# A gated hybrid block on one core: a new written order, a refitted transfer model and 17 convolution taps moved from VectorE to ScalarE and adding transfers

## The chip, the core and the metric

The kernel runs on one core of a Trainium2 chip. The core has a matrix engine (TensorE, PE in the profile, whose weight loads the profile lists apart as PEld), three engines for elementwise work (VectorE = DVE, ScalarE = ACT, GpSimd = POOL) and SyncE (SP), which here only issues transfers. Each engine works through its own queue in order; an instruction that waits for another engine holds up everything behind it in its queue. The metric is the device time of one execution in microseconds (us).

## The reference

One decoder layer for 256 tokens with 16 meta tokens in front (272 rows), width 2048, float32:

```
u = rms_norm(h, g_pre_mix)
z_pool | v_conv | g_conv | gate_a | gate_b = split(u @ w_in)     # 1024 | 1024 | 1024 | 2048 | 2048 columns
y_a = causal_multiscale_pool(z_pool, w_grp, scale) @ w_pool_out
y_b = conformer_conv(v_conv, g_conv, ...) @ w_conv_out           # a = v*sigmoid(g); 31 causal taps per channel; LayerNorm; silu
m = sigmoid(gate_a) * y_a + sigmoid(gate_b) * y_b
h = h + rms_norm(m @ w_o, g_post_mix)
f = square(relu(rms_norm(h, g_pre_mlp) @ w_up)) @ w_down         # 2048 -> 8192 -> 2048
out = (h + rms_norm(f, g_post_mlp))[16:]
```

## The kernel before

**Products.** A weight matrix is read in chunks of 1 MB (128 partitions x 2048 numbers). Precision comes from splitting: ScalarE rounds a chunk to `hi` (L816), VectorE subtracts to get the rest, `lo` (L821), and each product is made of three matmuls: weight hi with activation hi and lo, and weight lo with activation hi. The chunk lands in a raw room by a transfer that SP issues (L795). There are three pairs of `hi` and `lo`, used in turn, so the `hi` of a product can be written only when the product three places earlier has ended on PE.

**Stages.** Zones come first: eight column strips of `w_in` for z (pool), v and g (convolution), two chunks each, in the order g0, v0 and then the table `AFTER_G0` (L34). From v and g of a zone h come two channel tiles of `a = v*sigmoid(g)` (L939), and from them the convolution: tap 0 with the bias by ScalarE (L944), then for each of the other 30 taps a pair of VectorE instructions that add `tap * shifted a` onto `c` (L951). Then `grp`, the small product of the pool branch, whose result ScalarE (L1069) and VectorE (L1072) take out of the banks as `y`. After it come the products that the table `MAIN` (L36) lists, one word each.

**Words.** `p` is the pool projection, `a` gate a, `b` gate b, `c` the conv projection, `o` is `w_o`. `a13` is the normal product of gate a, column block 1, row block 3: two halves of 12 matmuls, one for each 128 tokens. `a0P5` is one of the seven products of a Strassen scheme over the column blocks 0 and 1; it has 12 matmuls, but its weights are often a sum of two blocks. `T01` transposes a finished block; `fu` makes the Strassen sums of the activations u (L1395, L1165ff, L1177, L1179), `k1` frees a room, `lnm` and `lnv` are the LayerNorm's mean and variance, and the other words are side steps of the same kind.

**Sums of weight blocks.** P5, P6, P7 and P4 need the sum of two blocks. The table `SUMMED` (L42) names those for which both blocks are loaded and VectorE adds them (L833); for the others POOL issues a transfer that reads the second block from memory and adds it onto the first in its room (L837, called a bring here).

**Banks.** There are six PSUM banks for products, four named `bank_k` and two `acc_v`. A Strassen product that goes to two places is copied out by ScalarE (L1300), and a next product that adds into the same bank waits for that copy: in the order before, `a13` follows `a0P5` into the same bank.

**Who sets the order.** The order of PE is the written one. For the other engines the class `Plan` simulates the program: it gives each operation a due time, counted back from the PE product that needs it, and lets an engine take the ready operation with the earliest due time. Transfers have a model of their own: issue time, a moving time, and shares of the bandwidth between SP's and POOL's queues:

```
class Plan:      ISSUE = {"SP": (0.4, 1.09), "POOL": (1.28, 2.44)}; LANDS = 1.13; SHARE SP (1.0, 1.0, 1.0), POOL 3.55
class LoadedPlan: ISSUE = {"SP": (0.4, 1.36), "POOL": (1.28, 2.05)}; LANDS = 0.93; SHARE SP (1.0, 2.54, 4.08), POOL 3.66
```

`LoadedPlan` stands in the kernel before, but no plan uses it. A second plan (L1721) does the same for the MLP, where weights are split at L1799 and L1804, summed at L1816 and L1821, and half of a bank of up-products is taken out by ScalarE (L1876) and the other by VectorE (L1883).

**Moved taps.** `convolve` already has a way for taps that VectorE does not do: for the first `MOVED_TAPS[h]` taps of zone h, ScalarE multiplies both channel tiles into one of three buffers w (L957) and POOL issues a transfer of 256 KB inside the core's memory that adds the buffer onto `c` (L967). The buffers lie in the room S1, next to z. In the kernel before the table is empty. The step `fu` writes its sums into the same room, so its first instruction waits for whoever used it.

Of the kernel before, what the change touches and what calls it, by code (L numbers as in the profile page):

```python
# [30 lines left out]

DUMMIES = (11, 2, 1)
SQUARES_FROM = 5
AFTER_G0 = [("z", 0), ("z", 1), ("z", 2), ("z", 3), ("v", 1), ("g", 1), ("v", 2), ("g", 2),  # L34
            ("v", 3), ("g", 3)]
MAIN = (  # L36
# [5 lines left out]
SUMMED = {('gate0', 0): '67', ('gate0', 2): '57', ('gate1', 0): '5', ('co', 2): '46', ('o', 0): '46'}  # L42
MOVED_TAPS = {}


class Plan:
# [163 lines left out]
def hybrid_block(ctx: ExitStack, tc: tile.TileContext, ins: dict, out: bass.AP):  # L210
    nc = tc.nc
# [393 lines left out]
                self.tile = self.make()  # L605
            return self.tile

    plan = Plan()

    def on_vector(n, f, reads, writes, extra=0.0):  # L610
        plan.add("DVE", (n + 151) / 960 - 0.083 + extra, f, reads=reads, writes=writes, late=0.1)
# [170 lines left out]
    def loads():  # L782
        while to_load:
            r = to_load[0]
            ends_ = uses[last_use[r]][0]
            fit = [q for q in free_rooms if index_of.get(q, len(products)) > ends_]
            if not fit:
                return
            to_load.pop(0)
            q = room_at[r] = fit[0]  # L790
            free_rooms.remove(q)
            src, (rows, _) = source(r)

            def f(q=q, src=src, rows=rows):
                nc.sync.dma_start(rooms[q]().rearrange("p (k c) -> p k c", k=rows), src)  # L795
            if early[0]:
                early[0] -= 1
                f()
            else:
                plan.add("SP", 3.06 if r[0] in ZONES else 2.87, f, writes=(f"raw{q}",))  # L800

    slot0 = at["slot"] - 1
    split_at = [dict() for _ in products]
# [21 lines left out]
    def weights(m_):  # L825
        while done_uses[0] < len(uses) and uses[done_uses[0]][0] <= m_:
            n = done_uses[0]
            done_uses[0] += 1
            w, what, raws_, extra = uses[n]
            at_rooms = [room_at[r] for r in raws_]  # L830
            names = [f"raw{q}" for q in at_rooms]
            if what == "sum":
                plan.add("DVE", 2.22, lambda a=at_rooms[0], b=at_rooms[1]: nc.vector.tensor_add(  # L833
                    rooms[a](), rooms[a](), rooms[b]()), reads=names, writes=names[:1], late=0.13)
            elif what == "bring":
                src, (rows, _) = source(extra)
                plan.add("POOL", 4.94, lambda a=at_rooms[0], src=src, rows=rows: nc.gpsimd.dma_start(  # L837
                    rooms[a]().rearrange("p (k c) -> p k c", k=rows), src, accum_op=ALU.add),
                    reads=names, writes=names)
            else:  # L840
                high, low = split_of(w, at_rooms[0], source(raws_[0])[1][0])
                h_, l_ = half_names(w)
                plan.add("ACT", 1.82, high, reads=names, writes=(h_,), late=0.13)
                plan.add("DVE", 2.22, low, reads=names + [h_], writes=(l_,), late=0.13)
            for r in raws_:
                if last_use[r] == n:
                    free_rooms.append(room_at[r])
            loads()
# [869 lines left out]
    banks["b"] = misc_tile("bank_b")  # L1718
    ov = out[0].rearrange("(t p) d -> p t d", p=P)

    plan = Plan()  # L1721
    steps = []
    for i in range(NP):
        text = FIRST_PIECE if i == 0 else PIECE if i < NP - 1 else LAST_PIECE
# [504 lines left out]
```

## Time and profile before

| | |
|---|---|
| median of 3 runs | 1186.25 us (1184.76 to 1186.58) |
| profiled execution | 1186.12 us |
| its span in the profile | 1184.0 us, 15794 instructions |
| granted TensorE clock, mean | 0.996 |
| PE busy | 1168.2 us (99%) |
| DVE / ACT / POOL busy | 1062.6 / 707.1 / 63.6 us |

The profiled execution lies 0.13 us under the median, and 2.12 us of it lie outside the span. A row of a timeline gives the start, the duration, the engine, the line, the operation, what is written from what, how many instructions are grouped, and in brackets the idle time before them with what ended it. The view of waits sums these idle times by the one who waited and the one waited for. In the chain of work each row is followed back to what released it, so its rows add up to the span. `PE acc_v L1251` is the matmul of a main product into an `acc_v` bank.

### The profile page before, as it was taken

Reading aid. Unit: us, or ns where it says so; the run is one execution under the profiler, and the core shown is the slowest. Engines: PE = TensorE matmul, PEld = TensorE weight load, DVE = VectorE, ACT = ScalarE, POOL = GpSimd, SP = SyncE. Lnnn points to the kernel's source line nnn. Section 1 sums busy time; section 2 is a strip of 40 time slices with the busy share of each in tenths; the row PEclk is TensorE's granted clock in tenths of the full one; section 3 lists DMA queues with packets and bytes.
Section 4 is the critical chain, followed back from the end, with each engine's and each line's share of the span. In section 5 each row is a group of like instructions: output and inputs, shape, how many; then the busy total and the mean of one; then the engine's idle time right before and its main releaser. Section 6 shows DMA issues by size and latency. Waiting matters only on the chain.

```text
span 1184.0 us, 15794 instructions
## 1 busy us (share of the span) xinstructions
PE 1168.2 (99%) x6314; PEld 1013.8 (86%) x6314; DVE 1062.6 (90%) x1154; ACT 707.1 (60%) x718; POOL 63.6 (5%) x63
## 2 busy tenths in 40 slices
PE   9999999999999999999999999999999999999996
PEld 9999988788888888898888888888888888888885
DVE  6799999999989999687998998998989989989856
ACT  7634354565479666466776665666656756656632
POOL 1000000000000000000101001000000010010000
PEclk9999999999999999999999999999999999999998
DMA  9855355898868799449999999999998999999931
GB/s 313 262 181 180 107 168 175 232 295 277 238 188 258 235 323 334 129 155 333 254 317 233 250 314 259 252 286 245 302 262 228 342 233 249 311 253 247 323 137 71
DMA packets 185705, 288.62 MB, mean 244 GB/s; under 512 B 4785, under 2 KB 92273, under 8 KB 184720
## 3 DMA queue, kind: packets, MB, share of 16 engines
q1 hardware_dynamic: 160496, 235.88, 58.0%
q0 software_dynamic: 24384, 50.49, 23.7%
q10 hardware_dynamic: 752, 1.25, 0.3%
q8 instruction: 49, 0.80, 0.3%
q14 instruction: 24, 0.20, 0.0%
HBM read 283.41 MB, written 4.19 MB: 243 GB/s over the span
## 4 chain that ended last, share of the span: by engine, by line
PE 89%; DVE 5%; DMA 3%; ACT 1%; issue 1%; DVEq 0%; POOL 0%; POOLq 0%; ACTq 0%; SPq 0%
PE bank_k L1251 18%; PE bank_u L538 16%; PE acc_up L1978 12%; PE acc_v L1251 9%; PE bank_u L544 8%; PE bank_a L1978 7%; PE bank_k L533 6%; PE bank_b L1978 5%; PE acc_v L533 3%; DVE c L951 2%; DVE lo L821 1%; DMA kept<-h 1%; PE acc_v L1511 1%; PE bank_u L1978 1%; DMA raw_h<-in_w_up_dram 1%
## 5 line engine op out<-in xcount | busy, mean ns | idle before, releaser
L538 PE MATMUL bank_u<-m,hi 128*128 128x512 f32 x960 | 329.9, 390 | 0.7 <-DVE F_raw L1883 0.7
L544 PE MATMUL bank_u<-m,lo 128*128 128x256 f32 x960 | 265.4, 276 | 0.0
L538 PEld LDWEIGHTS bank_u<-m,hi 128*128 128x128 f32 x960 | 180.2, 188 | 38.9 <-DVE F_raw L1883 1.0
L816 ACT CAST hi<-raw_p 128x2048 fp32r<-128x2048 f32 x70 | 133.8, 1913 | 116.5 <-PE bank_k L533 23.5
L1804 DVE TENSOR_TENSOR lo<-raw_m,hi 128x2048 fp32r<-128x2048 f32 x75 | 171.6, 2288 | 18.8 <-ACT hi L1799 17.7
L544 PEld LDWEIGHTS bank_u<-m,lo 128*128 128x128 f32 x960 | 180.2, 188 | 1.6
L1799 ACT CAST hi<-raw_m 128x2048 fp32r<-128x2048 f32 x75 | 143.4, 1913 | 60.2 <-PE bank_u L538 38.8
L821 DVE TENSOR_TENSOR lo<-raw_p,hi 128x2048 fp32r<-128x2048 f32 x70 | 159.6, 2287 | 16.3 <-ACT hi L816 16.0
L1978 PE MATMUL acc_up<-hi,forms 128*128 128x512 f32 x440 | 143.9, 390 | 0.2 <-ACT G L2003 0.2
L1804 DVE TENSOR_TENSOR lo<-raw_h,hi 128x2048 fp32r<-128x2048 f32 x43 | 98.4, 2287 | 13.3 <-ACT hi L1799 13.1
L1799 ACT CAST hi<-raw_h 128x2048 fp32r<-128x2048 f32 x43 | 82.1, 1910 | 40.5 <-PE bank_u L538 17.8
L951 DVE SCALAR_TENSOR_TENSOR c<-a,taps,c 128x256 f32<-128x256 f32 x240 | 100.3, 479 | 0.0
L1978 PEld LDWEIGHTS acc_up<-hi,forms 128*128 128x128 f32 x440 | 82.6, 188 | 18.4 <-ACT G L2003 0.6
L533 PE MATMUL bank_k<-u_um,hi 128*128 128x272 f32 x512 | 95.2, 287 | 0.0
L1251 PE MATMUL bank_k<-hi,u_um 128*128 128x512 f32 x280 | 88.8, 389 | 0.0
L1978 PE MATMUL acc_up<-lo,forms 128*128 128x512 f32 x220 | 85.9, 391 | 0.0
L1978 PE MATMUL bank_a<-hi,forms 128*128 128x512 f32 (+1 forms) x256 | 81.9, 383 | 0.0
L533 PEld LDWEIGHTS bank_k<-u_um,hi 128*128 128x128 f32 x512 | 79.7, 188 | 0.0
L533 PE MATMUL bank_k<-u_um,lo 128*128 128x272 f32 x256 | 73.3, 287 | 0.0
L1799 ACT CAST hi<-raw_c 128x2048 fp32r<-128x2048 f32 x23 | 43.9, 1908 | 42.0 <-PE bank_u L538 37.1
L1804 DVE TENSOR_TENSOR lo<-raw_c,hi 128x2048 fp32r<-128x2048 f32 x23 | 52.6, 2286 | 13.2 <-ACT hi L1799 13.2
L1978 PE MATMUL bank_b<-hi,forms 128*128 128x512 f32 (+1 forms) x200 | 63.5, 381 | 0.0
(384 smaller groups left out, 2228.8 us busy)
## 6 DMA issues: line engine op xcount, KB each, us to landing
raw_p<-in_w_in_dram SPq DMA_DIRECT2D x32, 1024.0 KB, 5.3
raw_m<-in_w_down_dram SPq DMA_DIRECT2D x25, 1024.0 KB, 8.7
raw_m<-in_w_down_dram POOLq DMA_DIRECT2D x23, 1024.0 KB, 10.3
raw_h<-in_w_up_dram SPq DMA_DIRECT2D x20, 1024.0 KB, 8.0
raw_m<-in_w_up_dram SPq DMA_DIRECT2D x17, 1024.0 KB, 8.5
raw_h<-in_w_down_dram SPq DMA_DIRECT2D x17, 1024.0 KB, 8.9
raw_c<-in_w_down_dram SPq DMA_DIRECT2D x15, 1024.0 KB, 5.1
raw_a<-in_w_up_dram SPq DMA_DIRECT2D x13, 1024.0 KB, 8.2
```

Of the source, the lines that this page charges most:

```text
L533: nc.tensor.matmul(acc, w[:, k[0], cs], act[:, k[1], a, off:], start=first and n == 0, stop=last and n == 2)
L538: nc.tensor.matmul(acc.rearrange("p (a t) -> p a t", a=2)[:, :, ts], hi[:, k[0], cs], act[:, k[1], :, off + ts.start:off + ts.stop], start ...
L544: nc.tensor.matmul(acc[:, :T], lo[:, k[0], cs], act[:, k[1], 0, off:], start=False, stop=stop, skip_group_check=True)
L816: nc.scalar.copy(box["flat"], rooms[q]())
L821: nc.vector.tensor_sub(lo, rooms[q](), f32(box["flat"]))
L951: nc.vector.scalar_tensor_tensor(C_c()[:, q, :], A_a()[:, q, i:i + T], taps[:, q, i:i + 1], C_c()[:, q, :], op0=ALU.mult, op1=ALU.add)
L1251: nc.tensor.matmul(banks[bank], a_(k, part), box[w_][:, k, :], start=opens and k == 0 and i == 0, stop=ends_ and k == CK - 1 and i == 2, s ...
L1511: nc.tensor.matmul(acc, act(kk)(a_, half(t)), w_[:, k, :], start=kk == 0 and n == 0, stop=kk == nk - 1 and n == 2, skip_group_check=True)
L1799: nc.scalar.copy(box["flat"], raw_in(room))
L1804: nc.vector.tensor_sub(lo, raw_in(room), f32(box["flat"]))
L1978: nc.tensor.matmul(acc, forms[h][:, f, k, a_, :], box[w_][:, k, cs], start=start and k == 0 and n == 0, stop=stop and k == KH - 1 and n == ...
```

## The change

Six tables and costs are changed; no instruction is written in another way.

- Both plans use `LoadedPlan`, with costs of 3.15 and 2.95 in place of 3.06 and 2.87 for SP's loads and 5.38 in place of 4.94 for a bring.
- `AFTER_G0`: the strip z3 moves from before v1 to behind v2.
- `MAIN`: the same 96 words in another order.
- `SUMMED`: P6 of gate a's second pair goes from a bring to a VectorE sum, and in the pairs of `w_conv_out` and `w_o` another two of the four are summed.
- `MOVED_TAPS`: 4 taps of zone 1 and 13 of zone 2 go the way of L957 and L967.

```diff
-AFTER_G0 = [("z", 0), ("z", 1), ("z", 2), ("z", 3), ("v", 1), ("g", 1), ("v", 2), ("g", 2),
+AFTER_G0 = [("z", 0), ("z", 1), ("z", 2), ("v", 1), ("g", 1), ("v", 2), ("z", 3), ("g", 2),
             ("v", 3), ("g", 3)]
 MAIN = (
-    "p00 p01 p30 p31 p21 p20 fu p10 p11 k1 a0P1 a0P2 a2P1 a0P5 a13 a12 a0P6 a0P3 a0P7 a02 a0P4 "
...
+    "p00 p30 p31 fu p11 p20 p10 p01 p21 k1 a0P1 a0P2 a0P5 a2P1 a12 a2P2 a0P6 a0P3 a0P7 a03 a0P4 "
...
-SUMMED = {('gate0', 0): '67', ('gate0', 2): '57', ('gate1', 0): '5', ('co', 2): '46', ('o', 0): '46'}
-MOVED_TAPS = {}
+SUMMED = {('gate0', 0): '67', ('gate0', 2): '567', ('gate1', 0): '5', ('co', 2): '67', ('o', 0): '67'}
+MOVED_TAPS = {1: 4, 2: 13}
...
-    plan = Plan()
+    plan = LoadedPlan()
...
-                plan.add("SP", 3.06 if r[0] in ZONES else 2.87, f, writes=(f"raw{q}",))
+                plan.add("SP", 3.15 if r[0] in ZONES else 2.95, f, writes=(f"raw{q}",))
...
-                plan.add("POOL", 4.94, lambda a=at_rooms[0], src=src, rows=rows: nc.gpsimd.dma_start(
+                plan.add("POOL", 5.38, lambda a=at_rooms[0], src=src, rows=rows: nc.gpsimd.dma_start(
...
-    plan = Plan()
+    plan = LoadedPlan()
     steps = []
```

Counted over the whole program, VectorE has 34 tap instructions fewer (206 for 240) and one weight sum more (10 for 9), ScalarE has 34 multiplications more, and POOL issues 17 adding transfers of 256 KB more and one bring fewer (10 for 11). SP's loads stay 240 and PE's instructions 6309, of the same kinds. In the MLP the orders of PE, SP and POOL stay as they were; only VectorE's and ScalarE's change, by a few places near its start. Lines of the changed kernel are one higher than before from L44 on.

**At grp (VectorE).** Before, from the last taps ahead of grp's results on; `acc_v` and `bank_k` hold those results, and `lo_1875` belongs to the second product after grp:

```order
L951 SCALAR_TENSOR_TENSOR c<-a,taps,c 128x256 x4
L821 TENSOR_TENSOR lo_1875<-raw_p_414,hi_1847 128x2048
L1072 SCALAR_TENSOR_TENSOR y<-acc_v_0_169,vecs,y 128x256
L1072 SCALAR_TENSOR_TENSOR y<-acc_v_1_170,vecs,y 128x256
L1072 SCALAR_TENSOR_TENSOR y<-bank_k_406,vecs,y 128x256
L1072 SCALAR_TENSOR_TENSOR y<-bank_k_407,vecs,y 128x256
```

The changed kernel at the same place, where `lo_1913` is that product's:

```order
L952 SCALAR_TENSOR_TENSOR c<-a,taps,c 128x256 x4
L1073 SCALAR_TENSOR_TENSOR y<-acc_v_0_169,vecs,y 128x256
L1073 SCALAR_TENSOR_TENSOR y<-acc_v_1_170,vecs,y 128x256
L1073 SCALAR_TENSOR_TENSOR y<-bank_k_406,vecs,y 128x256
L1073 SCALAR_TENSOR_TENSOR y<-bank_k_407,vecs,y 128x256
L822 TENSOR_TENSOR lo_1913<-raw_p_414,hi_1859 128x2048
L1073 SCALAR_TENSOR_TENSOR y<-bank_k_408,vecs,y 128x256
```

Four of grp's results now stand ahead of the `lo`, two behind it.

**At the first products of gate a (ScalarE, then POOL).** Before, from the `hi` of a0P1 (`hi_2163`) on; `hi_2201` is a0P2's, `hi_2241` a2P1's, `hi_2263` a0P5's, `hi_2283` a13's and `hi_2299` a12's; the copy of a0P5's bank is the one from `acc_v_1_170`:

```order
L816 CAST hi_2241<-raw_p_414 128x2048
L1219 COPY ya<-bank_k_407 128x512
L816 CAST hi_2263<-raw_p_412 128x2048
L1300 COPY sg_2265<-bank_k_408 128x512
L816 CAST hi_2283<-raw_p_413 128x2048
L816 CAST hi_2299<-raw_k_2239 128x2048
L1300 COPY sg_2265<-acc_v_0_169 128x512
L1300 COPY sg_2265<-acc_v_1_170 128x512
```

The changed kernel; `hi_2272` is a0P5's, `hi_2289` a2P1's, `hi_2293` a12's, `hi_2326` a2P2's, and a0P5's bank is `bank_k_406`:

```order
L817 CAST hi_2272<-raw_p_412 128x2048
L817 CAST hi_2289<-raw_p_414 128x2048
L817 CAST hi_2293<-raw_p_413 128x2048
L1301 COPY sg_2309<-acc_v_0_169 128x512
L1301 COPY sg_2309<-bank_k_406 128x512
L817 CAST hi_2326<-raw_k_2262 128x2048
L1301 COPY sg_2309<-bank_k_407 128x512
```

The copy that the product after a0P5's bank needs now stands ahead of the split of `raw_k`, not behind it, and a2P1 lies between the two on PE.

POOL before, from the clearing of `a` on, and then changed; `raw_p_412` holds a0P1's block, onto which the first bring adds for a0P5:

```order
L892 MEMSET a 128x8x14
L837 DMA raw_p_412<-in_w_in_dram 128x4x512 x2
L837 DMA raw_p_414<-in_w_in_dram 128x4x512 x2
L837 DMA raw_p_413<-in_w_in_dram 128x4x512
L837 DMA raw_p_414<-in_w_in_dram 128x4x512 x2
```

```order
L893 MEMSET a 128x8x14
L968 DMA c<-z 128x512 x17
L838 DMA raw_p_412<-in_w_in_dram 128x4x512 x2
L838 DMA raw_p_414<-in_w_in_dram 128x4x512
L838 DMA raw_p_412<-in_w_in_dram 128x4x512
```

The 17 tap transfers stand ahead of the first bring.

**At the start of the MLP (VectorE).** Before; `bank_u` holds up-products:

```order
L1804 TENSOR_TENSOR lo_4875<-raw_a,hi_4851 128x2048
L1883 TENSOR_TENSOR F_raw<-half_1_4873,bank_u_4483 128x256
L1816 TENSOR_TENSOR raw_m_4481<-raw_m_4481,raw_m_4480 128x2048
L1804 TENSOR_TENSOR lo_4896<-raw_m_4479,hi_4892 128x2048
L1883 TENSOR_TENSOR F_raw<-half_1_4894,bank_u_4484 128x256
L1804 TENSOR_TENSOR lo_4919<-raw_m_4481,hi_4915 128x2048
```

The changed kernel:

```order
L1805 TENSOR_TENSOR lo_4871<-raw_a,hi_4868 128x2048
L1884 TENSOR_TENSOR F_raw<-half_1_4891,bank_u_4500 128x256
L1956 TENSOR_TENSOR forms_4490<-F_raw,forms_4490 128x4x128
L1817 TENSOR_TENSOR raw_m_4498<-raw_m_4498,raw_m_4497 128x2048
L1956 TENSOR_TENSOR forms_4491<-F_raw,forms_4491 128x4x128
L1884 TENSOR_TENSOR F_raw<-half_1_4911,bank_u_4501 128x256
L1805 TENSOR_TENSOR lo_4934<-raw_m_4496,hi_4909 128x2048
L1805 TENSOR_TENSOR lo_4936<-raw_m_4498,hi_4932 128x2048
```

The second L1883 (L1884 now) stands ahead of a `lo` that it stood behind, and two steps of L1955 have come in between.

More of the change, by code (lines that the diff above doesn't have):

```diff
@@ L33 @@
 SQUARES_FROM = 5
-AFTER_G0 = [("z", 0), ("z", 1), ("z", 2), ("z", 3), ("v", 1), ("g", 1), ("v", 2), ("g", 2),
+AFTER_G0 = [("z", 0), ("z", 1), ("z", 2), ("v", 1), ("g", 1), ("v", 2), ("z", 3), ("g", 2),
             ("v", 3), ("g", 3)]
 MAIN = (
[5 rows of a table removed]
-SUMMED = {('gate0', 0): '67', ('gate0', 2): '57', ('gate1', 0): '5', ('co', 2): '46', ('o', 0): '46'}
-MOVED_TAPS = {}
[5 rows of a table added]
+)
+SUMMED = {('gate0', 0): '67', ('gate0', 2): '567', ('gate1', 0): '5', ('co', 2): '67', ('o', 0): '67'}
+MOVED_TAPS = {1: 4, 2: 13}
 class Plan:
```

8 rows, old and new, of the table MAIN are left out of this document.

## The prediction

> **What bounds the kernel.** I read the page's busy times first, then PE's waits, then busy times by stage, and the chain and timelines only at the places where PE waits.
>
> ```profile
> span 1184.0 us, 15794 instructions
> PE 1168.2 (99%) x6314; PEld 1013.8 (86%) x6314; DVE 1062.6 (90%) x1154; ACT 707.1 (60%) x718; POOL 63.6 (5%) x63
> ```
>
> PE is the bound. The change leaves its instructions as they are in number and kind, so it can win only what PE waits, and can lose without such a limit. The waits of PE (who waited, for whom, us in total, times, longest):
>
> ```profile
> PE acc_v L1251 <- ACT sg L1300: 1.9, 1, 1.9
> PE idle L450 <- POOL ident masks.py:199: 1.4, 1, 1.4
> PE bank_u L538 <- DVE F_raw L1883: 0.7, 1, 0.7
> PE acc_v L533 <- DVE y L1072: 0.4, 1, 0.4
> PE acc_up L1978 <- ACT G L2003: 0.2, 1, 0.2
> ```
>
> The second lies in the start-up, which isn't touched. The other four make 1.9 + 0.7 + 0.4 + 0.2 = 3.2 us, and that is the most a new order can take off. Busy time by stretches (start and end, length, each engine's busy time, clock, DMA share, GB/s) shows where they lie:
>
> ```profile
> 24.00:156.80 132.80, 132.80 (x1076) 132.39 (x1077) 125.08 (x202) 60.36 (x62) 0.19 (x1) 1.00 0.58 186
> 156.80:163.30 6.50, 6.10 (x50) 5.90 (x49) 6.50 (x13) 5.48 (x10) 0.00 (x0) 1.00 0.53 179
> 163.30:206.80 43.50, 43.50 (x193) 35.99 (x193) 43.50 (x73) 22.07 (x21) 1.37 (x1) 1.00 0.58 180
> 206.80:219.60 12.80, 10.90 (x50) 8.68 (x48) 11.60 (x15) 9.58 (x8) 0.00 (x0) 1.00 0.91 289
> 219.60:375.90 156.30, 156.30 (x688) 129.09 (x689) 148.31 (x151) 95.82 (x80) 8.93 (x7) 1.00 0.82 239
> ```
>
> The zones (first row), the pool products (third) and the rest of the gates (last) run with PE never waiting; the 0.4 us is at grp (second row), the 1.9 us at the first products of gate a (fourth). VectorE is full in rows two and three, but nothing there waits for it beyond the 0.4.
>
> **The 0.4 us at grp.** VectorE takes grp's results out of the banks behind a split:
>
> ```profile
> 158.85 2.29 DVE L821 TENSOR_TENSOR lo<-raw_p,hi 128x2048 fp32r<-128x2048 f32 x1
> 161.05 0.87 DVE L1072 SCALAR_TENSOR_TENSOR y<-acc_v,vecs,y 128x256 fp32r<-128x256 f32 x2
> ```
>
> In the new order four of these results come first. The split's product is the second after grp, so 2.29 us later is still in time. The term is −0.4, as long as ScalarE, whose half of each result comes first, isn't held up by a tap ahead of it (see the tap chain).
>
> **The 1.9 us at a13.** The chain of work (start, length, what):
>
> ```profile
> 195.94 10.89 PE bank_k L1251 x48
> 206.85 9.43 DMA raw_k<-in_w_in_dram
> 216.67 1.91 ACT hi L816
> 218.58 0.97 ACT sg L1300 x2
> ```
>
> The load of `raw_k` starts when the last pool product ends; ScalarE's split of it waits for the landing, and the copy that frees a0P5's bank waits behind the split. Now the copy stands ahead of that split, a2P1 fills 2.7 us between a0P5 and a12, and `raw_k` is first used one product later, by a2P2. The term is −1.9.
>
> **A new wait at a0P5.** This is the term I am least sure of. a0P5 needs a0P1's block with a second one added by a bring, and the rows of before give its whole path:
>
> ```profile
> 195.98 1.92 ACT L816 CAST hi<-raw_p 128x2048 fp32r<-128x2048 f32 x1 [2.13 <-PE acc_v L1251]
> 198.38 2.29 DVE L821 TENSOR_TENSOR lo<-raw_p,hi 128x2048 fp32r<-128x2048 f32 x1
> 200.97 1.37 POOL L837 DMA_DIRECT2D raw_p<-in_w_in_dram  x1 [164.31 <-DVE lo L821]
> 210.09 1.91 ACT L816 CAST hi<-raw_p 128x2048 fp32r<-128x2048 f32 x1 [0.83 <-DMA raw_p<-in_w_in_dram]
> 212.12 2.29 DVE L821 TENSOR_TENSOR lo<-raw_p,hi 128x2048 fp32r<-128x2048 f32 x1
> 212.10 0.39 PE L1251 MATMUL acc_v<-hi,u_um 128*128 128x512 f32 x1
> 214.82 0.39 PE L1251 MATMUL acc_v<-hi,forms_u 128*128 128x512 f32 x1
> DMA to landing us min/median/max: 8.3/9.0/9.7
> ```
>
> The first split cannot start earlier, because its buffer is free only when the sixth of the eight pool products ends. In before the `lo` was ready at 214.41 and a0P5 began at 214.82, its second matmul, the first to read `lo`, 0.23 us behind it. Now a0P5 stands where a2P1 began, 214.82 − 212.10 = 2.72 us earlier: its second matmul is due at 212.32. The first `lo` need not sit behind eight taps now (six stand ahead of it) and can start at 197.90; then it ends at 200.19, the bring starts at 200.5, lands 9.1 us later as here, and 1.91 + 2.29 us and short gaps follow: 213.85. The wait is 1.5 us. With the fastest landing of the last row, 8.3, it is 0.7; with the slowest, 9.7, and the `lo` no earlier than before, it is 2.7. I take 1.5, since this very transfer took 9.1 in this place, beside the same kind of SP loads. [...]
>
> **The tap chain.** Each of the 13 tap transfers of zone 2 adds onto the same `c`, so each waits for the one before. The room the buffers lie in is taken by `fu`'s sums on VectorE, right behind a0P1's `lo`, at about 200.2. The second half of zone 2's `a` is ready at 137.8, and its products have as many ahead of them as before:
>
> ```profile
> 137.37 0.43 DVE L939 TENSOR_TENSOR a<-v,g 128x272 f32<-128x272 f32 x1
> L944 ACT ACTIVATE c<-a,vecs,taps 128x256 f32<-128x256 f32 x8 | 4.7, 594 | 4.2 <-DVE a L939 4.2
> L951 DVE SCALAR_TENSOR_TENSOR c<-a,taps,c 128x256 f32<-128x256 f32 x240 | 100.3, 479 | 0.0
> q0 software_dynamic: 3696, 7.34, 29.7%
> raw_p<-in_w_in_dram POOLq DMA_DIRECT2D x7, 1024.0 KB, 9.2
> 457.42 0.57 POOL L1444 DMA_DIRECT2D g_mix<-in_g_post_mix_dram  x1 [15.84 <-issue]
> out_dram<-F_raw ACTq DMA_DIRECT2D x1, 256.0 KB, 2.4
> taps_in<-in_w_dw_dram POOLq DMA_DIRECT2D x1, 124.0 KB, 6.6
> ```
>
> Two ScalarE multiplications (nearest row L944, 0.59 us) and an issue put the first at 139.1, so 13 transfers have 200.2 − 139.1 = 61.1 us, or 4.7 each. No row of before shows such a transfer. An estimate: in the 145 us from 195 on, seven brings kept the DMA engines 29.7% busy, 6.15 us each, and took 9.2 to land, so 3.05 us are not moving. A quarter of 6.15 is 1.54; a transfer of whole rows is issued in 0.57 instead of 1.27 us; 0.3 for waking POOL (the bring's issue at 200.97 came so long after its `lo` at 200.67) makes 4.2. The ends are 2.4 (256 KB going out) and 6.6 (124 KB, POOL's queue). At 4.2 the last lands at 193.7, and the chain costs nothing. Beyond 4.7 every 0.1 costs 1.3 us, at 6.6 some 25. Beyond much the same value grp's results are late too, since ScalarE holds the seventh tap of zone 2 ahead of them until the fourth transfer has landed; that isn't added, as what PE loses there moves the chain's deadline along.
>
> Zone 1's four taps end long before zone 2 begins. The 34 multiplications (34 x 0.59, at most 20 us) fall on ScalarE, which is 60% busy. VectorE loses 34 x 0.42 (100.3 / 240), 14 us, and gains one sum of 2.3. That wins nothing by itself: PE doesn't wait for the convolution.
>
> ```profile
> 319.89 0.42 DVE L1082 TENSOR_TENSOR v<-v,c 128x256 f32<-128x256 f32 x1
> 334.18 0.59 PE L1094 MATMUL bank_y<-v,ones 128*128 128x256 f32 x2
> ```
>
> The last sum for the mean is done 14 us before PE uses it. In the new order that use comes some 6.5 us earlier and the work is 12 us less, so the cover stays. The moved z3 lies in the zones, where PE never waits: nothing.
>
> **The other order of products and sums.** Among the gates the loads of blocks for a sum now stand closer to their use: counted by these durations, a0P3 (its `lo` stands on VectorE behind a0P7's sum, which needs a second load) and a03 have 0 to 0.3 us to spare, the rest 2 us and more. I put 0 on it, between 0 and +1.
>
> **The MLP's start.** VectorE's second half-bank:
>
> ```profile
> 571.98 0.41 DVE L1883 TENSOR_TENSOR F_raw<-half,bank_u 128x256 f32<-128x256 f32 x1
> 574.51 2.28 DVE L1804 TENSOR_TENSOR lo<-raw_m,hi 128x2048 fp32r<-128x2048 f32 x1
> 576.71 0.41 DVE L1883 TENSOR_TENSOR F_raw<-half,bank_u 128x256 f32<-128x256 f32 x1
> ```
>
> It now comes ahead of the 2.28 us split, so the 0.7 goes; but that split is then late by 0.6 us for two steps of L1955, of which its product bears most. I take −0.5, between −0.7 and +0.3.
>
> **The sum.** −0.4 − 1.9 + 1.5 + 0 + 0 − 0.5 = −1.3. The profiled execution goes from 1186.12 to 1184.8; it lies 0.13 under the median, so the median goes from 1186.25 to 1184.9, or −0.11%. A difference under 0.2% (2.4 us) can hardly be told from none here, so this counts as the same.
>
> **The rivals.**
> - *The bring is early enough.* If it lands in under 8 us, a0P5 waits 0.4 or less, and with the MLP's 0.7 gone the sum is −0.4 − 1.9 + 0.4 − 0.7 = −2.6: 1183.6, just faster; at most −3.2, 1183.0. For it speaks that the bring can start 0.5 us earlier; against it that none of this line landed under 8.3.
> - *The tap chain is too slow (the slower side).* At 5.1 us a transfer, 13 x 0.4 = +5.2 come on top of −1.3: 1190.2. It decides from 5.0 on, where 13 x 0.3 passes 2.4 + 1.3. For it speaks that the chain is strictly serial and that 6.6 stands in the trace; against it that the 6.6 falls into the start, when all loads begin.
> [...]
> - *Late blocks among the gates.* a0P3, a03 or a32 wait for a load or a sum, +1 to +4: 1186 to 1189.
>
> **How the numbers follow.** The forecast, 1184 to 1187 with small misses, 0.39; the early bring 0.36; the slow tap chain 0.14, the starved one 0.02; late blocks 0.09, half of it within 0.2%. So faster 0.36, same 0.43, slower 0.21. From 1182.8, below which the waits of before leave almost nothing, the range reaches to a tap transfer of 5.1 us, 1190.2, and leaves out the slower chains.
>
> **What would show it.** PE's waits lose the entries on L1300, L1072 and L1883 (one line higher now); a new one on `lo` of about 1.5 us stands near 212. The tap transfers show a median of 4.2 us to landing, the last before 195, and VectorE has no idle time ahead of L1396. A landing above 4.7 with VectorE idle there, or PE waiting for grp's banks at 158 to 163, proves the forecast wrong on the slow side; a0P5 on time, on the fast side.

## The result, and the profile after

The changed kernel takes 1197.34 us (median of 5, 1194.41 to 1204.51) where the kernel before, beside it, takes 1186.08: a ratio of 1.0103, with a 95% interval of 1.0087 to 1.0118. It is 1% slower. The forecast was 1184.9, and the range ended at 1190.2. Timed once more on another occasion the ratio was 1.0058 (1.0036 to 1.0080), from executions between 1188.6 and 1199.4: the changed kernel scatters by some 10 us, where the one before scatters by 2 to 6.

The page of the changed kernel, whose lines are one higher than before:

```profile
span 1197.6 us, 15834 instructions
PE 1174.0 (98%) x6314; PEld 1017.5 (85%) x6314; DVE 1052.3 (88%) x1121; ACT 720.3 (60%) x752; POOL 76.8 (6%) x79
```

The span is 13.6 us longer; this execution, of 1199.38 us, lies 2 us above the median. PE's waits:

```profile
PE bank_k L1252 <- ACT ya L1220: 3.1, 2, 2.2
PE acc_v L1252 <- DVE lo L822: 3.1, 1, 3.1
PE bank_k L1252 <- DVE lo L822: 2.0, 1, 2.0
PE acc_v L534 <- DVE y L1073: 1.4, 1, 1.4
PE idle L451 <- POOL ident masks.py:199: 1.4, 1, 1.4
PE bank_k L1252 <- ACT hi L817: 0.5, 1, 0.5
PE acc_up L1979 <- ACT G L2004: 0.4, 1, 0.4
PE bank_k L1252 <- DVE forms_o L1180: 0.4, 1, 0.4
```

Without the start-up's 1.4 they make 10.9 us, 7.7 more than before. PE is also busy 1174.0 − 1168.2 = 5.8 us longer with the same instructions, and 7.7 + 5.8 = 13.5 is the whole difference. Where that lies (start and end, length, busy times of PE, PEld, DVE, ACT and POOL, clock, DMA share, GB/s):

```profile
156.80:166.00 9.20, 7.77 (x59) 7.27 (x58) 8.16 (x17) 6.29 (x13) 1.39 (x2) 1.00 0.68 171
166.00:206.00 40.00, 36.85 (x155) 29.73 (x154) 32.37 (x55) 21.95 (x27) 5.49 (x7) 0.96 0.76 205
206.00:219.00 13.00, 10.30 (x46) 8.20 (x44) 8.29 (x10) 4.60 (x6) 2.18 (x2) 1.00 0.81 178
219.00:231.00 12.00, 9.05 (x24) 6.64 (x25) 12.00 (x14) 7.23 (x6) 0.00 (x0) 0.72 0.76 264
```

All of it lies between grp and a0P5. The clock, 1.00 there before, is 0.96 over 40 us and 0.72 over 12: (1 − 0.96) x 40 + (1 − 0.72) x 12 = 5.0 us lost, most of the 5.8. VectorE is idle for 7.6 of the 40 us of the pool products, where it had no idle time before. The chain of work runs through the tap transfers here:

```profile
178.57 7.16 DMA c<-z
...
186.27 3.27 DMA c<-z
...
200.53 7.04 DMA c<-z
...
208.09 5.17 DMA c<-z
...
213.49 1.90 DVE q_u L1396 x3
```

The first tap transfer of zone 2 is issued at 140.4 and the last lands at 213.3, so one of the 13 takes 5.6 us from issue to issue, not 4.2: 5.1 to its landing in the mean, and 0.5 more until the next is issued. Over all 17, shortest, median and longest from issue to landing:

```profile
DMA to landing us min/median/max: 3.2/4.7/7.9
```

### The profile page after: what moved, and what is told of

The parts are those of the page before. It is cut to its first block, busy times and chain, and to the rows that moved or that the text cites. A ratio compares the mean times of both kernels' runs of the same rounds, so it can differ in the third digit from the quotient of the medians.

```text
span 1197.6 us, 15834 instructions
## 1 busy us (share of the span) xinstructions
PE 1174.0 (98%) x6314; PEld 1017.5 (85%) x6314; DVE 1052.3 (88%) x1121; ACT 720.3 (60%) x752; POOL 76.8 (6%) x79
## 4 chain that ended last, share of the span: by engine, by line
PE 76%; DMA 5%; DVE 3%; ACT 2%; issue 1%; DVEq 0%; ACTq 0%; POOLq 0%
PE bank_u L539 17%; PE bank_k L1252 13%; PE acc_up L1979 12%; PE bank_u L545 9%; PE acc_v L1252 8%; PE bank_a L1979 7%; PE bank_b L1979 5%; DMA c<-z 3%; PE acc_up L539 1%; DMA raw_um<-in_w_o_dram 1%; PE bank_u L1979 1%; DMA raw_h<-in_w_up_dram 1%; ACT hi L817 1%; DVE lo L1805 1%; PE acc_up L545 1%
## 5 line engine op out<-in xcount | busy, mean ns | idle before, releaser
L1805 DVE TENSOR_TENSOR lo<-raw_m,hi 128x2048 fp32r<-128x2048 f32 x75 | 171.5, 2288 | 18.5 <-ACT hi L1800 17.3
L817 ACT CAST hi<-raw_p 128x2048 fp32r<-128x2048 f32 x68 | 129.6, 1909 | 83.5 <-PE bank_k L1252 18.2
L822 DVE TENSOR_TENSOR lo<-raw_p,hi 128x2048 fp32r<-128x2048 f32 x68 | 155.3, 2287 | 26.1 <-ACT hi L817 25.5
L1805 DVE TENSOR_TENSOR lo<-raw_h,hi 128x2048 fp32r<-128x2048 f32 x43 | 98.3, 2287 | 13.2 <-ACT hi L1800 12.8
L952 DVE SCALAR_TENSOR_TENSOR c<-a,taps,c 128x256 f32<-128x256 f32 x206 | 86.4, 477 | 1.1 <-DMA c<-z 1.1
L1252 PE MATMUL bank_k<-hi,u_um 128*128 128x512 f32 x208 | 66.4, 390 | 0.0
L1805 DVE TENSOR_TENSOR lo<-raw_c,hi 128x2048 fp32r<-128x2048 f32 x23 | 52.6, 2286 | 13.2 <-ACT hi L1800 13.2
```

The source lines that it names most:

```text
L817: nc.scalar.copy(box["flat"], rooms[q]())
L822: nc.vector.tensor_sub(lo, rooms[q](), f32(box["flat"]))
L952: nc.vector.scalar_tensor_tensor(C_c()[:, q, :], A_a()[:, q, i:i + T], taps[:, q, i:i + 1], C_c()[:, q, :], op0=ALU.mult, op1=ALU.add)
L1252: nc.tensor.matmul(banks[bank], a_(k, part), box[w_][:, k, :], start=opens and k == 0 and i == 0, stop=ends_ and k == CK - 1 and i == 2, s ...
L1805: nc.vector.tensor_sub(lo, raw_in(room), f32(box["flat"]))
```

## The experiments

Two theories stood at the start. A: the chain of tap transfers is the loss. B: the new order, the new sums and the new transfer model are. Ratios are to the kernel before on the same chip, with their 95% intervals.

**1. No taps moved.**

```diff
-MOVED_TAPS = {1: 4, 2: 13}
+MOVED_TAPS = {}
```

> The changed kernel with no tap moved (all 240 tap instructions on VectorE again); order, sums and the transfer model stay as changed. Theory A (the chain of tap transfers is the whole loss, the rest is what the prediction's sum says of it): 1184 to 1186 us, and PE's waits hold no ya (L1220) and no y (L1073) of over 0.5 us; a wait on lo at a0P5 of 0.7 to 2.7 us stays. Theory B (the new order and sums cost it): 1192 us or more, with PE waiting for lo, hi or banks among the gates as now.

Measured: 1187.75 us, 1.0013 (1.0003 to 1.0023), above theory A's 1184 to 1186 and far below B's 1192. So the taps are the loss, but the rest is no gain either. Its waits of PE:

```profile
PE bank_y L1095 <- DVE v L1083: 2.7, 1, 2.7
PE bank_k L1252 <- DVE lo L822: 1.4, 2, 1.1
PE idle L451 <- POOL ident masks.py:199: 1.4, 1, 1.4
PE bank_u L545 <- DVE lo L1805: 0.9, 1, 0.9
PE acc_up L1979 <- ACT G L2004: 0.6, 1, 0.6
PE acc_v L1252 <- DVE lo L822: 0.3, 1, 0.3
```

The waits at grp and at the bank of a0P5 are gone, a0P5 waits for its `lo` (the 1.1; counted from the pace of PE before it, its second matmul starts 1.3 us late), and at the mean PE waits 2.7 us for VectorE's sum of the convolution. A wait of that kind did not exist before.

**2. The taps alone, on the kernel before.**

```diff
-MOVED_TAPS = {}
+MOVED_TAPS = {1: 4, 2: 13}
```

> The kernel before with MOVED_TAPS = {1: 4, 2: 13} alone. A: 8 us or more slower than before (1194 to 1200), with tap transfers of 4.5 us and more in the median and PE waiting for ya or lo between 180 and 230 us. B: within 3 us of before.

Measured: 1194.42, 1.0073 (1.0058 to 1.0088). A holds from this side too.

**3 and 4. Seven taps of zone 2; and the sums of fu freed from the tap buffers.**

```diff
-MOVED_TAPS = {1: 4, 2: 13}
+MOVED_TAPS = {1: 4, 2: 7}
```

> The changed kernel with 7 taps of zone 2 moved, not 13. At 5.6 us each the seventh lands near 180, ahead of the sums of fu. A: the wait of VectorE at L1396 is gone, grp's late results (about 1.4 us) stay since the seventh tap still stands ahead of them on ScalarE: 1186 to 1188 us. B: 1195 or more. If ScalarE's queue behind the taps were worth nothing: 1185.

Measured: 1191.16, 1.0050 (1.0035 to 1.0065), between A's 1186 to 1188 and B's 1195. PE no longer waits at a0P2, but 2.4 us at grp for `y` and 1.3 just ahead of it for a `g`, while zone 2's chain is still running: a loss that I hadn't counted.

```diff
-    S1_z = Lazy("s1", [P, KP * L + 3 * 2 * T], "z")
-    S1_q = Lazy("s1", [P, 2, CK * CW], "q_u")
+    S1_z = Lazy("s1", [P, 2 * CK * CW], "z")
+    S1_q = lambda: S1_z().rearrange("p (a c) -> p a c", a=2)
...
-        plan.take(["raw10"] + names, names_z + names_w)
+        plan.take(["raw10"], names_z + names_w)
+        plan.take(names, names_z)
```

> The changed kernel with all 17 taps moved, but the sums of fu lie beside the tap buffers in room S1 and do not wait for them (z and the buffers keep their places). Takes away the wait at L1396 alone. If that wait (3.1 + 2.0 + 0.5 us of PE's waits less the 1.5 that a0P5 waits anyway, and two stretches of half clock, 1.7 us each) is the larger part: 1189 to 1191 us, with ya and y still waited for. If ScalarE's splits behind the taps are the larger part: 1193 to 1196.

Measured: 1192.75, 1.0062 (1.0044 to 1.0081), between the two expectations. The sums of fu now run far ahead, at 137 to 143 us in the zones, and still a0P5 waits 4.7 us: VectorE's next taps wait for the last landing until 210.3 and stand ahead of a0P2's split, and 14 more stand ahead of a0P5's. The room of fu is one hold and VectorE's queue another, and freeing the first uncovers the second.

**5 and 10. Zone 1's four taps only; and three.** With three buffers none of three multiplications has to wait for a transfer.

```diff
-MOVED_TAPS = {1: 4, 2: 13}
+MOVED_TAPS = {1: 4}
```

> The changed kernel with only zone 1's 4 taps moved. Without any moved tap PE waited 2.7 us for VectorE's sum of the convolution at the mean (plus half a stretch of half clock). Four pairs of tap instructions less are 4 x 0.83 = 3.3 us of VectorE. Theory: the taps serve that wait, and zone 1's chain is hidden: 1183 to 1185.5 us, wait at the mean under 0.5. Rival (zone 1's chain costs too, by ScalarE's splits waiting behind it): 1187 or more.

```diff
-MOVED_TAPS = {1: 4, 2: 13}
+MOVED_TAPS = {1: 3}
```

> The changed kernel with 3 taps of zone 1 moved and none of zone 2. With three buffers none of the three multiplications waits for a transfer, so no split on ScalarE stands behind a landing; VectorE's own taps of that zone still wait for the third landing. If ScalarE's held queue is what zone 1's four taps cost (VectorE idle 8 us between 100 and 125 for 3.3 us of work saved): VectorE's idle there falls under 4 us and the time is 1185 to 1189. If the wait of VectorE's taps for the transfers is the cause: 1191 or more, idle as with four.

Measured: 1193.52, 1.0070 (1.0055 to 1.0086) with four, and 1190.56, 1.0040 (1.0026 to 1.0054) with three, which lies between its two expectations. My theory for four was the reverse, that zone 1's taps help. The busy times from 100 to 125 us, without moved taps, with four and with three:

```profile
100.00:125.00 25.00, 25.00 (x205) 25.00 (x204) 24.96 (x43) 8.25 (x5) 0.00 (x0) 1.00 0.40 128
```

```profile
100.00:125.00 25.00, 25.00 (x205) 25.00 (x204) 16.46 (x23) 11.82 (x14) 3.51 (x4) 1.00 0.66 174
```

```profile
100.00:125.00 25.00, 25.00 (x205) 25.00 (x204) 19.62 (x28) 10.83 (x12) 2.65 (x3) 1.00 0.57 160
```

Four moved taps save VectorE 4 x 0.83 = 3.3 us and idle it for 8.5. With three it idles 5.4, though no multiplication waits. VectorE's timeline with three:

```profile
111.21 2.29 DVE L822 TENSOR_TENSOR lo<-raw_s0a,hi 128x2048 fp32r<-128x2048 f32 x1 [1.09 <-ACT hi L817]
117.13 2.29 DVE L822 TENSOR_TENSOR lo<-raw_s0a,hi 128x2048 fp32r<-128x2048 f32 x1 [3.63 <-ACT hi L817]
...
119.70 1.67 DVE L952 SCALAR_TENSOR_TENSOR c<-a,taps,c 128x256 f32<-128x256 f32 x4
```

The view names ScalarE's splits, but they come when PE frees their buffers, as ever. What is missing is the work that filled the time between: the moved taps are the first of their zone, so the other 26 or 27 can't begin before the last of them has landed, at 119.67, and zone 0's taps are used up. At the mean PE waits 5.1 us with four and 4.2 with three.

**17. The same three taps as the last of their zone.**

```diff
-        for i in range(1, 1 + moved):
+        for i in range(1, TAPS - moved):
+            plan.add("DVE", 0.4 * nq, tap(i), reads=[f"a{q}" for q in on(q0, nq)],
+                     writes=[f"c{q}" for q in on(q0, nq)], late=0.1)
+        for i in range(TAPS - moved, TAPS):
             j = w_next[0] % 3
...
-        for i in range(1 + moved, TAPS):
-            plan.add("DVE", 0.4 * nq, tap(i), reads=[f"a{q}" for q in on(q0, nq)],
-                     writes=[f"c{q}" for q in on(q0, nq)], late=0.1)
```

> The changed kernel with three taps of zone 1 moved, as in e10, but as the last of the zone and not the first. If VectorE's taps waiting for the third landing are what costs: VectorE is busy 24 us or more of the 25 between 100 and 125, the wait at the mean falls from 4.2 us (with three taps first) and 2.7 (with none) to under 1, and the time is 1184 to 1187. If the transfers cost in another way (the loads beside them, ScalarE): 1189 or more, as in e10.

Measured: 1188.57, 1.0019 (1.0009 to 1.0029), above the 1184 to 1187 that I expected. The intervals of the three taps put first (1.0026 to 1.0054) and last touch at their ends, and the difference of 0.0021 is just clear of noise. VectorE is full again, and the wait at the mean is gone:

```profile
100.00:125.00 25.00, 25.00 (x205) 25.00 (x204) 24.96 (x43) 11.56 (x14) 0.00 (x0) 1.00 0.43 139
```

So the taps of zone 1 cost because they came first: put last, they can't be told from no moved taps at all (1.0013, 1.0003 to 1.0023). It isn't a gain over the kernel before; the transfers now run from 172 to 187 us, and a0P5 waits 1.8 + 1.0.

**9. Zone 2's 13 taps only.**

```diff
-MOVED_TAPS = {1: 4, 2: 13}
+MOVED_TAPS = {2: 13}
```

> The changed kernel with only zone 2's 13 taps moved. If the two zones' losses add to what the whole change loses over no taps (about 9.6 us, of which zone 1's four taps alone made 5.8): 1190 to 1192 us, grp's results in time, the wait at fu and a0P5 as before. If zone 2's chain is the whole loss whatever zone 1 does: 1195 or more.

Measured: 1194.28, 1.0062 (1.0046 to 1.0079), between the two expectations. Zone 2's chain is not the whole loss, and the losses of the zones (1.0070 and 1.0062, less 1.0013 each, 0.0106 together) don't add up neatly either: the two timings of the whole change give 0.0090 and 0.0045. That the losses partly hide behind each other is an argument, not shown.

**6 and 7. What a tap transfer costs.** Half the pool projection's loads, which leaves half of its weights old, and copies that don't add, which leaves those taps out of the convolution:

```diff
-            def f(q=q, src=src, rows=rows):
+            def f(q=q, r=r, src=src, rows=rows):
+                n = rows // 2 if r[0] == "po" else rows
-                nc.sync.dma_start(rooms[q]().rearrange("p (k c) -> p k c", k=rows), src)
+                nc.sync.dma_start(rooms[q]().rearrange("p (k c) -> p k c", k=rows)[:, :n], src[:, :n])
```

> The changed kernel, in which the eight loads of the pool projection's weights fetch the first half of their rows (512 KB); the other half of the room keeps old numbers, so that projection is computed from wrong weights. Splits, products and tap transfers stay. Theory (a tap transfer is 3.2 us alone and longer by what SP's loads move beside it): the 13 transfers of zone 2 take 4.3 us or less in the mean, not 5.1, the last lands before 205 us, and the time is 1189 to 1193. Rival (their own price, whatever runs beside): mean landing within 0.3 of the changed kernel's, 1196 or more.

```diff
-                C_c()[:, q0:q0 + nq, :], w_view(j), accum_op=ALU.add),
+                C_c()[:, q0:q0 + nq, :], w_view(j)),
```

> The changed kernel, in which the tap transfers copy the buffer onto c and do not add, so those taps are lost from the convolution. Queue, size, order and waits stay. If the adding is what costs (it reads and writes its target): a transfer alone lands in about 2.4 us, as 256 KB going out does, the chain of 13 is some 10 us shorter, 1188 to 1191. If the price is the fixed part and SP's loads beside it: alone 3.0 to 3.3 us, time within 2 us of the changed kernel.

Measured: 1189.75, 1.0032 (1.0013 to 1.0051), and 1188.34, 1.0025 (1.0013 to 1.0038). Shortest, median and longest landing with half loads, then with plain copies:

```profile
DMA to landing us min/median/max: 3.2/3.9/7.1
```

```profile
DMA to landing us min/median/max: 2.2/4.1/7.1
```

Both theories hold a part. The shortest landing is 3.2 us when the transfer adds and 2.2 when it copies; POOL issues it in 0.86 and 0.54 us. The longer ones have company: in the changed kernel the transfers issued at 120.7, 147.1 and 190.1, with no load in flight, took 3.2 us, the 13 that took 3.9 us or more had loads in flight for 3.0 us or more, and those of 170.1 and 200.5, with one or two loads in flight all the while, took 7.9 and 7.0. Over the chain the company is harder to see: with half loads the 13 landings of zone 2 have a mean of 4.3 us and the chain ends at 202.6, but with full loads the means are 5.1 in the changed kernel and 4.4 to 5.0 in experiments 8, 13 and 14, whose programs are the same up to a0P2, so half loads are not clear of the scatter. Plain copies lie below all of these, with 3.9 us and the end at 197.0, and VectorE no longer waits for fu's room.

**8, 13 and 14. The half clock.** PE's matmuls behind a wait, in the changed kernel:

```profile
215.68 0.61 PE L1252 MATMUL acc_v<-hi,u_um 128*128 128x512 f32 x2
219.44 0.62 PE L1252 MATMUL acc_v<-lo,u_um 128*128 128x512 f32 x1 [3.15 <-DVE lo L822]
219.86 1.05 PE L1252 MATMUL acc_v<-hi,u_um 128*128 128x512 f32 x2
...
223.43 0.40 PE L1252 MATMUL acc_v<-hi,u_um 128*128 128x512 f32 x1
```

A pair takes 1.05 us instead of 0.61 until 223; the granted clock was 0.50 from 219.67 to 223.09. I filled the two long waits with work that nobody reads:

```diff
+        fill = {("2", 0): 50, ("5", 0): 38}.get((s, n0), 0) if stage == "gate0" else 0
+
+        def keep_busy():
+            for _ in range(fill):
+                nc.tensor.transpose(banks["y0"][:, :P], ident, ident)
+        if fill:
+            on_tensor(0.05, keep_busy, (), ("y0",))
```

> The changed kernel with 50 small transposes into an unused bank ahead of a0P2 on PE and 38 ahead of a0P5, about 3 and 2.3 us of work that nobody reads, where PE waited 3.1 and 2.0 us. If PE's idle time is what brings the half clock behind it: the two stretches of half clock between 215 and 232 us go, 3.4 us less: 1193 to 1195 with the waits replaced by the work. If the half clock has another cause: same time as the changed kernel or up to 2 us more.

> The changed kernel once more, as the measure for the next run: 1194 to 1200 us, with a scatter of several us from one execution to the next, as the landings of the tap transfers vary.

> The changed kernel with 50 and 38 small transposes ahead of a0P2 and a0P5, beside the changed kernel on the same chip. If the half clock behind the waits is part of the loss: 3 us or more under e13. If it costs nothing in the end (the time is set by when blocks land and VectorE gets to them): within 1.5 us of e13.

Measured: filled 1197.02, 1.0105 (1.0088 to 1.0122), then side by side 1196.56, 1.0093 (1.0076 to 1.0110), against 1193.81, 1.0058 (1.0036 to 1.0080), for the changed kernel. Side by side the filled kernel lies above both expectations. In the traces the half clock between 215 and 232 us is gone (granted clock 1.00 from 219 to 231 in experiments 8 and 14, 0.72 in 13), but no time is won. The filling was sized by an estimate at 3 and 2.3 us and takes far more, here in experiment 14:

```profile
216.42 5.62 PE L1341 MATMUL bank_y<-ident 128*128 128x128 f32 x50
224.63 4.31 PE L1341 MATMUL bank_y<-ident 128*128 128x128 f32 x38
```

That is 9.9 us of work in the place of 5.6 us of waits, 4.3 too much, where the two stretches of half clock lose 1.7 us each. So this neither prices the half clock nor shows whether it can be had back.

**11, 15, 16 and 18. Can the 1.9 us of before be won at all?** On the kernel before, a13's half with the free bank goes first:

```diff
-        order_ = range(NT)
+        order_ = (1, 0) if (stage, n, kc) == ("gate0", 1, 3) else range(NT)
```

> The kernel before, with the two halves of a13 in the other order: first the tokens whose bank is free, so the copy of a0P5's bank has 2.7 us more. Theory: the 1.9 us go and nothing else moves: ratio 0.9984, 1183.5 to 1185 where before is 1185.5 to 1186. Rival (a12 or a later load becomes late in its place): ratio 0.9995 to 1.001.

Measured: 1185.18, 1.0000 (0.9991 to 1.0008). The wait on L1300 is gone, and another stands in its place at 244 us:

```profile
PE bank_k L1251 <- DVE lo L821: 1.6, 1, 1.6
```

```profile
234.44 2.28 DVE L821 TENSOR_TENSOR lo<-raw_k,hi 128x2048 fp32r<-128x2048 f32 x1
...
239.52 2.29 DVE L833 TENSOR_TENSOR raw_p<-raw_p,raw_k 128x2048 f32<-128x2048 f32 x1
241.72 4.49 DVE L821 TENSOR_TENSOR lo<-raw_p,hi 128x2048 fp32r<-128x2048 f32 x2
```

The same row of the kernel before:

```profile
242.18 4.48 DVE L821 TENSOR_TENSOR lo<-raw_p,hi 128x2048 fp32r<-128x2048 f32 x2
```

VectorE has no idle time from 231 to 246 and comes to this `lo` only 0.46 us earlier than before. The wait at a13 came from a copy behind a split, but it cost nothing: a PE that comes 1.9 us earlier finds VectorE's `lo` not ready. Two attempts took a sum off VectorE, and one moved taps as the last of their zones:

```diff
-SUMMED = {('gate0', 0): '67', ('gate0', 2): '57', ('gate1', 0): '5', ('co', 2): '46', ('o', 0): '46'}
+SUMMED = {('gate0', 0): '67', ('gate0', 2): '7', ('gate1', 0): '5', ('co', 2): '46', ('o', 0): '46'}
```

> The kernel before with a13's halves exchanged and P5 of gate a's second pair made by a bring in place of VectorE's sum of two loaded blocks. If the load and the sum ahead of a2P5 hold the 1.6 us at 242 us: that wait goes, 1183 to 1184.5 us where before is 1185.3. If VectorE's or the loads' pace in the stretch holds it: 1185 to 1187, with the wait at another product.

```diff
-SUMMED = {('gate0', 0): '67', ('gate0', 2): '57', ('gate1', 0): '5', ('co', 2): '46', ('o', 0): '46'}
+SUMMED = {('gate0', 0): '6', ('gate0', 2): '57', ('gate1', 0): '5', ('co', 2): '46', ('o', 0): '46'}
```

> The same with P7 of the first pair brought in place of summed, 2.3 us less of VectorE's work before 230 us, while the load and the sum ahead of a2P5 stay. If VectorE's pace holds the 1.6 us: 1183 to 1184.5. If a2P5's load and sum hold it: 1185 to 1187, the wait at 242 stays.

```diff
-MOVED_TAPS = {}
+MOVED_TAPS = {1: 3, 2: 3}
```

(with the loop of experiment 17; all three keep a13's halves exchanged)

> The kernel before with a13's halves exchanged and three taps of zone 1 and of zone 2 moved, as the last of their zone: 6 x 0.83 = 5 us less for VectorE before 206 us. If VectorE's pace put the 1.6 us at 242: ratio 0.9985, 1183 to 1185. If the loads put it there, or the second zone's transfers come in the way of the bring: 0.9995 or more.

Measured: 1188.93 and 1188.95, both 1.0027 (1.0016 to 1.0038 and 1.0013 to 1.0040), for the sums, and 1201.92, 1.0134 (1.0119 to 1.0150) for the taps; the first two lie above all that I expected. In both kernels with a sum less a wait of 1.1 us stays, at 247 and at 243, and another has come ahead of it (2.7 us on a `lo` at 229; 2.3 on a bank's copy at 235). The planner puts the work of the other engines in another order each time, so these two don't show what VectorE's relief alone is worth. With the taps last, zone 2's transfers run until 226.7 us and hold fu's room; VectorE's first sum of fu starts at 226.85:

```profile
PE acc_v L1251 <- ACT forms_u L1177: 16.1, 1, 16.1
```

Six moved taps cost 16 us there, and by this trace the room that the buffers share with fu is what costs it.

**12. The changed order without its waits.** No taps, the mean and the variance later, a0P5 behind a2P1, a12's halves exchanged:

```diff
-MOVED_TAPS = {1: 4, 2: 13}
+MOVED_TAPS = {}
...
-    "p00 p30 p31 fu p11 p20 p10 p01 p21 k1 a0P1 a0P2 a0P5 a2P1 a12 a2P2 a0P6 a0P3 a0P7 a03 a0P4 "
-    "a02 a2P5 a13 a33 a2P6 b0P1 a2P3 a2P7 a22 a32 a23 b0P5 a2P4 b30 b31 b32 b0P6 b13 b0P2 b12 lnm "
-    "b0P7 b33 b0P4 b03 lnv b21 b20 b02 b0P3 k0r b22 b23 um8 c2P1 c00 c01 c2P5 c11 T01 c10 c2P6 "
+    "p00 p30 p31 fu p11 p20 p10 p01 p21 k1 a0P1 a0P2 a2P1 a0P5 a12 a2P2 a0P6 a0P3 a0P7 a03 a0P4 "
+    "a02 a2P5 a13 a33 a2P6 b0P1 a2P3 a2P7 a22 a32 a23 b0P5 a2P4 b30 b31 b32 b0P6 b13 b0P2 b12 "
+    "b0P7 b33 lnm b0P4 b03 b21 lnv b20 b02 b0P3 k0r b22 b23 um8 c2P1 c00 c01 c2P5 c11 T01 c10 c2P6 "
-        order_ = range(NT)
+        order_ = (1, 0) if (stage, n, kc) == ("gate0", 1, 2) else range(NT)
```

> The changed kernel with no tap moved, the mean one product pair later (behind b33, and the variance behind b21), a0P5 behind a2P1 again, and the halves of a12 in the other order. Takes away the waits that were left without moved taps: 2.7 + 1.7 of half clock at the mean, 1.3 at a0P5. Theory: 4 to 6 us under the kernel with no taps, 1182 to 1184.5. Rival: later loads or the variance wait instead, 1186 or more.

Measured: 1188.72, 1.0035 (1.0024 to 1.0046). The wait at the mean is gone; in its place PE waits 2.7 us for a ScalarE step of gate a (L1211) near 250 and 1.3 in the MLP. No version of the study beats the kernel before.

## Why the prediction was wrong

By its steps:

- **The tap chain** was the step that failed, the term that the sum put at 0, and it failed in size, place and number of holds. The transfer was put at 4.2 us (3.9 to its landing and 0.3 to wake POOL) and its limit at 4.7; it is 5.6 (5.1 and 0.5), so the last landed at 213.3 and not at 193.7, and fu's first sum on VectorE, due at 200.2, began at 213.49. The estimate took the moving part from transfers that had loads beside them and divided by four, 1.54 us; but 256 KB took 3.2 us alone and up to 7.9 us beside loads of 1 MB in the changed kernel, so it took up to 4.7 us more there. The rival "the tap chain is too slow" had the mechanism and the rule (13 x 0.9 over the limit gives +11.7), but its 5.1 us were too short and its chance of 0.14 too small, and the range stopped there. That its 11.7 less the 1.3 come near the 11.3 us of the first timing is luck in part: the second timing gives 7.7, zone 1's four taps, which the rule leaves out, cost 0.57% (6.8 us) alone, and with fu freed from the buffers the loss is still 0.62%.
- **"Zone 1's four taps end long before zone 2 begins"** was true (landed at 124, zone 2 starts at 140) and beside the point. I asked who waits for the last transfer and not what VectorE does meanwhile. It idled 8.5 us for 3.3 saved (experiment 5), and with three taps, putting them last took the idle time away (10 and 17).
- **"That wins nothing by itself: the cover stays"** at the mean: with all 17 taps moved PE does not wait there, as forecast, but it comes 8 us later than before to this place, and 6 us of cover are left. Without moved taps it waits 2.7 us (experiment 1). The use is due 6.2 us earlier than before, much as the prediction said, but VectorE's last sum is done 10.3 us later, at 330.62 against 320.31, and that was not counted. So in the new order PE does wait for the convolution, and taking taps off VectorE could win up to these 2.7 us.
- **Queues past which the taps were moved.** ScalarE's splits and copies behind the multiplications were counted at grp only; the copies at the pool products (L1220) cost 3.1 us. ScalarE's queue also makes the wait at a0P5: the bring landed at 219.59, but the split of its block began only at 222.36, since fu's casts (L1178) stand ahead of it and wait for the sums that the room held up. POOL's own queue did no harm, though 17 transfers stand ahead of the bring in it. The bring went out 0.3 us behind the end of a0P1's `lo`, as in the kernel before; the `lo` itself came 8.6 us later than forecast, 6.5 with the split ahead of it (202.51 against 195.98), which waits for a pool product on PE, and 2.1 behind taps on VectorE:

```profile
206.49 2.28 DVE L822 TENSOR_TENSOR lo<-raw_p,hi 128x2048 fp32r<-128x2048 f32 x1
209.06 1.32 POOL L838 DMA_DIRECT2D raw_p<-in_w_in_dram  x1
```

- **The half clock** behind PE's waits, 5.0 us, was not in the sum at all. In the trace of before no wait longer than 1.9 us stands in this stretch and the clock stays at 1.00.
- **−0.4 at grp**: right with no taps moved (experiment 1 has no such wait), 1.4 with them. It is the row that the prediction named and left out of the sum: ScalarE's seventh tap of zone 2 waits for the fourth landing (159.48), a split follows, and ScalarE takes grp's first result only at 161.77:

```profile
159.56 0.51 ACT L958 ACTIVATE z<-a,taps 128x256 f32<-128x256 f32 x1 [1.72 <-DMA c<-z]
159.98 1.90 ACT L817 CAST hi<-raw_p 128x2048 fp32r<-128x2048 f32 x1
161.77 0.83 ACT L1070 ACTIVATE y<-acc_v,vecs 128x256 fp32r<-128x256 f32 x2
```

- **−1.9 at a13**: the wait went as said, and was worth nothing (experiment 11). VectorE, full from there to 246 us, made PE wait 1.6 us at its `lo` 25 us later instead. The bound "PE can win what PE waits" was right as a bound; taking it as a gain was not.
- **+1.5 at a0P5**: right where no tap of zone 2 is moved: the second matmul starts 1.3 us late with none moved and 1.5 with three of zone 1. In the changed kernel PE waits 0.5 + 2.0 us there, for the other reason given above. The bring, put at 9.1 us, took 8.7 in experiment 1 and 10.5 in the changed kernel.
- **0 among the gates**: right. With no taps moved PE waits 0.3 us twice there.
- **−0.5 in the MLP**: the 0.7 went in the changed kernel, but 0.9 to 1.3 us on the neighbouring `lo` (L1805) came in three of the variants (1, 9 and 12), so the step is not worth a sure gain.
- **The starved chain**, with its chance of 0.02: no run shows it. In the changed kernel POOL issues a tap transfer in 0.85 to 0.93 us throughout, 0.86 at 155.2 us with VectorE in a split all the while and 0.86 at 190.1 with VectorE idle.

What stays open: how much of the loss is the half clock, how the two zones' losses overlap, and what a VectorE with less work would win where the orders of the other engines stay. That the scatter from one execution to the next comes from the landings is likely, but not shown: the filled kernel (experiments 8 and 14) had its last tap landing at 203.9 us in one profiled execution, with a span of 1190.8, and at 211.8 in another, with 1197.7, and these are two executions on two chips.

## What to carry to other kernels

Work that is moved to another engine by transfers can pay in the queues, not in the engines' busy time (here VectorE was busy 10.3 us less, 1052.3 for 1062.6, and the kernel took 11.3 us longer): count for each moved step the in-order queue it is put in, what stands behind it there, and what the relieved engine has left to do while the transfers run. Put moved parts of an accumulation last, so that the rest can go on (1.0019 for 1.0040 in experiments 17 and 10), but not so late that their buffers hold a room that someone needs (a wait of 16.1 us in experiment 18). And where a second engine is full, removing a short wait of the bounding engine can give nothing (1.0000 in experiment 11): the bounding engine only comes earlier to the next result that isn't ready. Here a new written order also changes the planner's order of every other engine: of the five small edits meant to remove one wait (experiments 11, 12, 15, 16, 18), each brought another of 1.6 us or more.

## What the runs showed of the hardware

- In the changed kernel an adding transfer of 256 KB inside the core's memory landed in 3.2 us with no other transfer beside it (three of the 17, issued at 120.7, 147.1 and 190.1); the shortest plain copy of the same took 2.2 (experiment 7). Beside loads of 1 MB the adding transfer took up to 7.9 us in the changed kernel, and the loads, 5.0 to 5.3 us alone (eleven, issued from 48.5 to 133.3), took up to 8.5 (issued at 176.0) with tap transfers and other loads beside them.
- Three stretches of half clock in the changed kernel, 3.4 us each at a granted clock of 0.50 by the trace's clock records (from 192.4, 219.7 and 226.5 us), come with PE waits of 1.0 and 2.2, of 3.1, and of 0.5 and 2.0 us. A lone wait of 1.9 us in the kernel before and one of 2.7 in experiment 12 were followed by none (granted clock 1.00, before from 206 to 235 us, in experiment 12 from 235 to 320). Behind one of 2.7 in experiment 15 eleven matmuls took 4.25 us, where twelve took 2.73 a little later, so PE was slow there. In the 16 us wait of experiment 18 the half clock began after some 4 us (granted clock 1.00 from 206 to 219 and 0.51 from 219 to 231), and the first twelve matmuls behind it took 5.53 us, the next twelve 2.76. Which length of wait brings it is not shown.
- GpSimd issued an adding transfer of 256 KB in 0.85 to 0.93 us in the changed kernel, also while VectorE was full: 0.86 at 155.2 us beside a split and 0.86 at 160.0 beside taps.
